# Weight tiles of one decoder layer, placed at set distances modulo 256 bytes from the activation tiles

## The chip, the core and the metric

The kernel runs on one core of a Trainium2 chip. The metric is device time in microseconds. Before the change it is 843.34 us, the median of three runs from 843.05 to 843.76. The one profiled execution took 842.98 us; the span that its page and its trace show, from the first to the last instruction, is 840.8 us, and 2.2 us lie around it.

## The reference

One layer of a decoder on 512 tokens of width 1024, all in float32. It has three sublayers with residual adds, and a last norm:

```python
h = rms_norm(x, norm_mix)
q, k, v, u, gate_b, gate_c, g_a, g_b = split(h @ w_in)
o_a = stick_breaking_attention(q, k, v)             # 8 heads x 64
y_b = gate_b * causal_depthwise_conv(gate_c * u)    # 3 taps, 512 channels
x = x + (sigmoid(g_a) * (o_a @ w_a) + sigmoid(g_b) * (y_b @ w_b)) @ w_mix_out
x = x + memory_cross_attention(rms_norm(x), rms_norm(mem), w_q, w_kv, w_o)   # 4 heads, 256 memory tokens
gate, up = split(rms_norm(x) @ w_ffn_in)            # 2 x 2816
x = x + (silu(gate) * up) @ w_ffn_out
return rms_norm(x, norm_final)
```

## The kernel before

**How a product is made.** Activations are kept transposed, channels on the 128 partitions and tokens along the row. Each float32 operand is split into a high and a low part, both in the matmul type float32r (`split` for activations, `halves`, `ffn_form` and `turn_form` for weights: ScalarE casts the high part, VectorE subtracts it). A product is then three matmuls: high by high, high by low, low by high (`mm3`, and the loop in `product`). Each matmul has a weight operand, 128 columns that are loaded into TensorE ahead of it, and a moving operand, which streams through. In the profile's rows `out<-moving,weights` stands for such a matmul, so `z<-xdh,wf` streams a tile `xdh` against weights `wf`; the instruction that loads the weights is the row of engine PEld with the same names.

**Two sizes.** Most plain products (`gemm`: the input projection `pr`, the branches `br`, the output projections `r` and `f`) stream 512 columns, all tokens of one part. The input half of the channel sublayer, the query projection of the memory sublayer, and four of the gate projections (`ffn_form`, `product`) use seven sums of 2 by 2 blocks in place of eight block products. Their matmuls stream 256 columns (`HS`), half of the tokens. There are 30 such units (22 of the channel sublayer, 4 of the query projection, 4 of the gates), each with seven products `i` = 0 to 6 of 4 slices by 3 matmuls: 84 matmuls a unit, 2,520 in all, all at line 802. The keys of the memory sublayer (`mem_k`) stream 256 columns too, the memory tokens: 8 calls of 8 slices by 3 matmuls, 192 in all. The products of `turn_form` and `turn_product` swap the roles: there the weight tile `tf` streams, 512 columns, and the activation forms are loaded.

**Where tiles lie.** Each pool takes a stretch of every partition's row. `upool` holds 52 units of 2,048 bytes: all activation parts `xgh`, `xoh`, `xch`, `acth` and so on. `wpool` holds four raw weights (`wr`), four high parts (`wh`) and four low parts (`wl`) of 4,096 bytes each; the block forms `wf` and `tf` use the buffers of `wh` and `wl`. `xpool` holds the forms `xdh` and `xdl` of the memory queries and of the channel sublayer; the gates' `xdh` and `xdl` are made by `pair_forms` with `split`, and so lie in `upool`. `lpool` holds the stick-breaking attention's `l` and `lq`, `cpool` the constants `ident`, `negtri`, `mean_r`. Start addresses in the built program, modulo 256 bytes:

| tiles | before | after the change |
|---|---|---|
| units in `upool` | 32 | 128 |
| `wh`, `wl` in `gemm`, `residual`, `mem_v`; `tf` | 32 | 128 |
| `wf` (block forms), `wh`, `wl` in `mem_k` | 32 | 192 |
| `xdh`, `xdl` in `xpool` | 64 | 128 |
| `l`, `lq` in `lpool` | 64 | 128 |
| `ident`, `negtri`, `mean_r` in `cpool` | 128 | 128 |

Slices of a tile start at multiples of 512 bytes, so each row of the table holds for all slices. Below, the distance of a matmul is the address of its weights less that of its moving operand, modulo 256. Counted over the built program, the 2,712 matmuls of line 802 and of `mem_k` divide before the change into 2,088 at distance 0 and 624 at distance 224, that is 32 bytes the other way (the 26 units whose `xdh` and `xdl` lie in `xpool`, 2 products of 12 matmuls each). Nearly all matmuls of 512 columns have distance 0 (2,022 of 2,062).

**What sets the order.** TensorE's order is written out by hand nearly everywhere (`manual_schedule`), in most of the kernel that of VectorE and ScalarE too. A form is made six products ahead of its use (`AHEAD`), its raw sums two more (`SUM_AHEAD`).

Of the kernel before, what the change touches and what calls it, by code (L numbers as in the profile page):

```python
# [8 lines left out]
F32 = mybir.dt.float32  # L9
F32R = mybir.dt.float32r  # L10
# [3 lines left out]
P = 128  # L14
D = 1024
S = 512
KD = D // P
TT = S // P
# [28 lines left out]
WARM = 8  # L47
FIRST = 4
LOADS_AHEAD = 6

O_Q, O_K, O_V, O_U, O_GB, O_GC, O_A, O_B = 0, 512, 1024, 1536, 2048, 2560, 3072, 4096

# [2 lines left out]
def hybrid_layer(ctx: ExitStack, tc: tile.TileContext, xT_d, memT_d, cols_d, wv_d, win_d,  # L55
# [3 lines left out]
    cpool = ctx.enter_context(tc.tile_pool(name="cpool", bufs=1))  # L59
    upool = ctx.enter_context(tc.tile_pool(name="upool", bufs=52))  # L60
    wpool = ctx.enter_context(tc.tile_pool(name="wpool", bufs=4))
    tpool = ctx.enter_context(tc.tile_pool(name="tpool", bufs=7))
    spool = ctx.enter_context(tc.tile_pool(name="spool", bufs=4))
# [9 lines left out]
    def nm(s):  # L73
        count[0] += 1
        return f"{s}{count[0]}"

    def unit(s, cols=512):
        return upool.tile([P, cols], F32R, tag="u", name=nm(s), padded_shape=[P, 512])

    def tmp(s, cols=512):  # L80
        return tpool.tile([P, cols], F32, tag="t", name=nm(s), padded_shape=[P, 512])

    def f(ap):
        return ap.bitcast(F32)

    def mmtile(s, pool=None, tag="mm"):
        return (pool or pmm).tile([P, 512], F32, tag=tag, name=nm(s))
# [21 lines left out]
    mean_r = cpool.tile([P, P], F32R, tag="mean_r", name="mean_r")  # L109
    nc.vector.tensor_copy(mean_r, mean_f)  # L110
    mean_sq = f(mean_r)
    eps_t = cpool.tile([P, 1], F32, tag="eps_t", name="eps_t", padded_shape=[P, 16])
    nc.vector.memset(eps_t, EPS)

    late_loads, n_loads = [], [0]
# [3 lines left out]
    def after(i, earlier):  # L119
        for e in earlier:  # L120
            tc.add_manual_dep(i.ins, e.ins.name, mybir.DependencyInfo(
                mybir.DependencyClass.NoSync, mybir.DependencyReason.DATA), reason="order")
# [28 lines left out]
    def chained(i):  # L151

        after(i, chain[-1:])
        chain.append(i)

    def load_w(src, cols=P):

        w, rest = halves(load_raw(src), D // cols)
        rest()
        return w  # L160

    def load_raw(src):
        raw = wpool.tile([P, D], F32, tag="wr", name=nm("wr"))
        i = nc.sync.dma_start(raw, src)
        loads[:] = [i]
        n_loads[0] += 1
        if n_loads[0] == LOADS_AHEAD + 1:
            after(i, late_loads[3:4])
        if count[1] < FIRST:
            count[1] += 1  # L170
            chained(i)
        return raw

    def halves(raw, k=KD):
        hi, lo = (wpool.tile([P, k, D // k], F32R, tag=t, name=nm(t)) for t in ("wh", "wl"))
        h2, l2 = (t.rearrange("p k c -> p (k c)") for t in (hi, lo))
        after(nc.scalar.copy(h2, raw), lead[-1:] + waiting[:1])  # L177

        def rest():
            lows.append(nc.vector.tensor_tensor(out=l2, in0=raw, in1=f(h2), op=ALU.subtract))  # L180
            after(lows[-1], waiting[1:])

        return (hi, lo), rest
# [6 lines left out]
    def gemm(ps, w, act, k0=0, ks=None):  # L190

        n = len(act)
        for k in ks or range(n):
            mm3(ps, (w[0][:, k0 + k, :], w[1][:, k0 + k, :]), act[k], k == 0, k == n - 1)
# [39 lines left out]
    def by_token_of(row, s):  # L234

        n = row.shape[1] // P
        r = cpool.tile([P, n, 32], F32, tag=s, name=nm(s))
        for g in range(TT):
            rows = slice(32 * g, 32 * g + 32)
            nc.vector.transpose(out=r[rows, :, :],  # L240
                                in_=row.rearrange("p (t c) -> p t c", c=P)[rows, :, rows])
        return r[:, :, 0]
# [20 lines left out]
    with tc.manual_schedule(engines={mybir.EngineType.Activation, mybir.EngineType.DVE}):  # L263
        for k in range(KD):
# [3 lines left out]
            if k == 0:  # L268
                hi, lo = unit("wvh"), unit("wvl")
# [36 lines left out]
    r0 = by_token_of(r0b, "r0")  # L306
# [9 lines left out]
    def open_project(col):  # L316
        w = load_w(win_d[col // P])
        ps = mmtile("pr")
        gemm(ps, w, xg, ks=range(KD // 2))
        opened.append((ps, w))  # L320
# [346 lines left out]
    def residual(w_dram, act, old, gain):  # L667
# [9 lines left out]
        def weight(m):  # L677
            if m not in raw:
                weight_raw(m)
            w[m], rest = halves(raw.pop(m))  # L680
            late.append(rest)
# [5 lines left out]
        def block(m, k0, k1, bank=mmtile):  # L687
            if k0 == 0:
                if m not in w:
                    w[m] = load_w(w_dram[m])  # L690
                ps[m] = bank("r")
            for k in range(k0, k1):
                mm3(ps[m], (w[m][0][:, k, :], w[m][1][:, k, :]), act[k], k == 0, k == KD - 1)
            if k1 == KD:
                finish(m)
# [39 lines left out]
    FORM_TAGS = "wh", "wl"  # L735
# [20 lines left out]
    def ffn_raw(m, i, eng=nc.vector):  # L756
        if m not in raws:
            ffn_load(m)
        w = raws[m]
        if w[i] is None:  # L760
            w[i] = fpool.tile([P, 512], F32, tag="w2", name=nm("s2"), bufs=4)
            a, b = (w[2], w[0]) if i == 3 else (w[3], w[1])
            eng.tensor_tensor(out=w[i], in0=a, in1=b, op=ALU.add)
        return w[i]

    wforms, made = {}, [0]

    def ffn_form(m, i, later=None):

        if (m, i) in wforms:  # L770
            return
        if i == 0:
            ffn_raw(m, i)
            pair = pairs[m]
            hi, lo = (wpool.tile([P, 2, 512], F32R, tag=t, name=nm("wf")) for t in FORM_TAGS)
            nc.scalar.copy(hi, pair)  # L776

            def rest():
                nc.vector.tensor_tensor(out=lo, in0=pair, in1=f(hi), op=ALU.subtract)  # L779

            if later is None:
                rest()
            else:
                later.append(rest)
            for j in range(2):
                wforms[m, j] = hi[:, j, :], lo[:, j, :]
            return
        raw = ffn_raw(m, i)
        w = wpool.tile([P, 2, 512], F32R, tag=FORM_TAGS[made[0] % 2], name=nm("wf"))
        made[0] += 1  # L790
        hi, lo = wforms[m, i] = w[:, 0, :], w[:, 1, :]
        nc.scalar.copy(hi, raw)  # L792
        nc.vector.tensor_tensor(out=lo, in0=raw, in1=f(hi), op=ALU.subtract)  # L793
# [139 lines left out]
    for n in range(GATE_AHEAD):  # L933
        ffn_form(*gs[n])
    with tc.manual_schedule(engines={mybir.EngineType.PE, mybir.EngineType.Activation,
# [7 lines left out]
        for n, (m, i) in enumerate(gs):  # L943
# [6 lines left out]
            if n + GATE_AHEAD < len(gs):  # L950
                ffn_form(*gs[n + GATE_AHEAD])
# [78 lines left out]
    km, vm, mq, scs, prs, pts = [], [[None] * 2 for _ in range(MT)], {}, {}, {}, {}  # L1030

    def mem_k(m):
        w = load_w(wmk_d[m])
        ps = mmtile("km")
        gemm(ps[:, :MEM], w, mg)
        t = tmp("km", MEM)
        nc.vector.tensor_tensor(out=t, in0=ps[:, :MEM], in1=rmb, op=ALU.mult)
        if m % 2 == 0:
            km_pair[:] = unit("kmh"), unit("kml")
        hi, lo = (u[:, (m % 2) * MEM:(m % 2 + 1) * MEM] for u in km_pair)  # L1040
        nc.scalar.copy(hi, t)
        nc.vector.tensor_tensor(out=lo, in0=t, in1=f(hi), op=ALU.subtract)
        km.append((hi, lo))
# [76 lines left out]
    with tc.manual_schedule(engines={mybir.EngineType.PE}):  # L1120
        for part, *args in ((mem_q, 0), (mem_k, 0), (mem_k, 1), (mem_scale,), (mem_k, 2), (mem_k, 3),
                            (mem_q, 1), (mem_scores, 0), (mem_k, 4), (mem_k, 5), (mem_scores, 1),
                            (mem_q, 2), (mem_k, 6), (mem_k, 7), (mem_turn, 0), (mem_v, 0),
                            (mem_turn, 1), (mem_scores, 2), (mem_q, 3), (mem_out, 0), (mem_out, 1),
                            (mem_v, 1), (mem_turn, 2), (mem_scores, 3), (mem_out, 2),
                            (last, 0, 0, 6), (last, 1, 0, 2), (mem_turn, 3), (last, 1, 2, 6),
                            (mem_out, 3), (last, 2, 0, 6, otile), (last, 0, 6, 8), (last, 1, 6, 8),
                            (last, 2, 6, 8)):
            part(*args)
        for m in range(3, KD):  # L1130
            last(m, 0, KD)
# [5 lines left out]
    def evict(m, part):  # L1137
# [6 lines left out]
        else:  # L1144
            a = act[m] = f(unit("act"))
            for half, u in enumerate((b["z"][:, :HS], b["t"][:, HS:])):
# [11 lines left out]

    rms, eps_sq = f(unit("rms")), cpool.tile([P, S], F32, tag="cu", name="eps_sq",
                                                 bufs=2, padded_shape=[P, S + 2])  # L1160
    eps_t4 = spool.tile([P, TT], F32, tag="epst", name="epst", bufs=1)
    eps_d = cpool.tile([P, P], F32, tag="eps_d", name="eps_d")
    yt = {}

    def turn_residual(t, h):
# [134 lines left out]

    def turn_form(p, i):

        w = wpool.tile([P, 2, 512], F32R, tag=FORM_TAGS[made[0] % 2], name=nm("tf"))
        made[0] += 1
        hi, lo = tforms[p, i] = w[:, 0, :], w[:, 1, :]
        nc.scalar.copy(hi, turn_raws[p][i])
        nc.vector.tensor_tensor(out=lo, in0=turn_raws[p][i], in1=f(hi), op=ALU.subtract)

    for k in range(TURN):
        w = load_w(wfo_d[k], D)  # L1310
# [63 lines left out]
    sums4 = {}  # L1374

    def small(s, cols=1):
        return spool.tile([P, cols], F32, tag=s, name=nm(s))

    def mean_part(t, j):

# [27 lines left out]
    rest = []  # L1408
# [123 lines left out]
```

## Time and profile before

| | |
|---|---|
| median of three runs | 843.34 us |
| profiled execution | 842.98 us |
| its span | 840.8 us |
| TensorE busy (weight loads apart) | 832.2 us, 5,077 matmuls |
| weight loads (PEld) | 744.9 us |
| VectorE busy | 678.3 us |
| ScalarE busy | 484.5 us |

In the page a row's time is the mean duration of one matmul, from when it starts to when its last result is out, and matmuls overlap: a matmul of 512 columns lasts 390 ns in these rows while the next one starts 227 ns after it. What one matmul costs is therefore read from the starts in the timeline, as a difference over several matmuls.

### The profile page before, as it was taken

The page shows a single profiled execution, that of the slowest core. Times are in us where ns is not written, and L with a number is a line of the kernel's source. Part 1 is how long each engine was busy: PE and PEld are TensorE (multiplying, and loading weights), DVE is VectorE, ACT ScalarE, POOL GpSimd, SP SyncE. Part 2 cuts the span into 40 slices and gives each one's busy share as a digit, 9 for nine tenths or more (in the row PEclk, how much of TensorE's full clock was granted, in tenths as well). Part 3 has the DMA queues.
Part 4 walks back from the last instruction along what each step waited for, and adds up shares of the span by engine and source line. Part 5 has one row for each costly group of instructions (what it writes and reads, how often), then busy time and mean ns, then how long its engine had stood idle before and what let it go on. Part 6 is the DMA issues. An engine that isn't in the chain of part 4 may idle for free.

```text
span 840.8 us, 13447 instructions
## 1 busy us (share of the span) xinstructions
PE 832.2 (99%) x5077; PEld 744.9 (89%) x5077; DVE 678.3 (81%) x1172; ACT 484.5 (58%) x874; POOL 85.2 (10%) x111
## 2 busy tenths in 40 slices
PE   9999999999999999999999999999999999999996
PEld 7888788888899988999988889999999999888885
DVE  8779889988866867988765889888877778889865
ACT  7466767666534555766554766555555556464534
POOL 1011112210100011000000111211111110010002
PEclk9999999999999999999999999999999999999999
DMA  8342232315645485565331437777777673881002
GB/s 301 108 144 82 95 101 72 105 51 183 192 110 141 155 241 152 142 182 195 129 112 62 113 81 206 185 184 183 180 176 176 176 176 113 266 273 51 1 1 101
DMA packets 50000, 119.67 MB, mean 142 GB/s; under 512 B 5136, under 2 KB 8208, under 8 KB 49936
## 3 DMA queue, kind: packets, MB, share of 16 engines
q1 hardware_dynamic: 40672, 101.23, 36.2%
q0 software_dynamic: 8976, 17.30, 12.4%
q8 instruction: 40, 0.66, 0.3%
q10 hardware_dynamic: 288, 0.29, 0.1%
q14 instruction: 24, 0.20, 0.1%
HBM read 115.63 MB, written 2.10 MB: 140 GB/s over the span
## 4 chain that ended last, share of the span: by engine, by line
PE 98%; DVE 1%; ACT 1%; issue 0%; DVEq 0%; ACTq 0%
PE z L802 20%; PE y L802 10%; PE pr L186 6%; PE pr L187 6%; PE pr L188 6%; PE v L802 5%; PE r L187 3%; PE r L186 3%; PE r L188 3%; PE v L302 3%; PE f L186 2%; PE f L188 2%; PE f L187 2%; PE t L188 2%; PE t L186 2%; PE t L187 2%
## 5 line engine op out<-in xcount | busy, mean ns | idle before, releaser
L177 ACT CAST wh<-wr 128x1024 fp32r<-128x1024 f32 x80 | 83.5, 1049 | 56.3 <-PE pr L187 10.1
L180 DVE TENSOR_TENSOR wl<-wr,wh 128x1024 fp32r<-128x1024 f32 x80 | 97.3, 1220 | 17.8 <-ACT wh L177 17.1
L802 PE MATMUL z<-xdh,wf 128*128 128x256 f32 x480 | 94.6, 281 | 0.0
L186 PE MATMUL pr<-xgh,wh 128*128 128x512 f32 x224 | 87.5, 391 | 0.0
L187 PE MATMUL pr<-xgl,wh 128*128 128x512 f32 x224 | 87.3, 390 | 0.0
L188 PE MATMUL pr<-xgh,wl 128*128 128x512 f32 x224 | 87.3, 390 | 0.0
L802 PEld LDWEIGHTS z<-xdh,wf 128*128 128x128 f32 x480 | 77.5, 189 | 0.2
L802 PE MATMUL z<-xdl,wf 128*128 128x256 f32 x240 | 67.0, 279 | 0.0
L826 ACT COPY sa<-z 128x256 f32<-128x256 f32 x52 | 19.4, 373 | 73.2 <-PE z L802 73.2
L793 DVE TENSOR_TENSOR wf<-s,wf 128x512 fp32r<-128x512 f32 x60 | 41.4, 692 | 22.6 <-ACT wf L792 21.4
L752 POOL DMA_DIRECT2D ws<-in_w_ffn_in_dram x22 | 26.5, 1206 | 299.7 <-DMA ws<-in_w_ffn_in_dram 123.6
L779 DVE TENSOR_TENSOR wf<-wg,wf 128x1024 fp32r<-128x1024 f32 x30 | 36.8, 1226 | 17.9 <-ACT wf L776 17.9
L188 PEld LDWEIGHTS pr<-xgh,wl 128*128 128x128 f32 x224 | 42.1, 188 | 8.8
L186 PEld LDWEIGHTS pr<-xgh,wh 128*128 128x128 f32 x224 | 42.1, 188 | 8.5 <-DVE rv L141 0.2
L187 PEld LDWEIGHTS pr<-xgl,wh 128*128 128x128 f32 x224 | 42.1, 188 | 8.3
L802 PE MATMUL y<-xch,wf 128*128 128x256 f32 x240 | 49.0, 286 | 0.0
L802 PE MATMUL z<-xch,wf 128*128 128x256 f32 x240 | 48.1, 283 | 0.0
L802 PEld LDWEIGHTS z<-xdl,wf 128*128 128x128 f32 x240 | 45.4, 189 | 0.2
L793 DVE TENSOR_TENSOR wf<-ws,wf 128x512 fp32r<-128x512 f32 x60 | 41.0, 683 | 1.8 <-ACT wf L792 1.7
L802 PE MATMUL v<-xoh,wf 128*128 128x256 f32 x208 | 42.0, 283 | 0.0
L802 PE MATMUL z<-xf,wf 128*128 128x256 f32 x312 | 41.8, 283 | 0.0
L802 PE MATMUL y<-xoh,wf 128*128 128x256 f32 x208 | 41.8, 284 | 0.0
(359 smaller groups left out, 2479.7 us busy)
## 6 DMA issues: line engine op xcount, KB each, us to landing
wr<-in_w_in_dram SPq DMA_DIRECT2D x28, 512.0 KB, 3.6
ws<-in_w_ffn_in_dram SPq DMA_DIRECT2D x22, 512.0 KB, 3.9
ws<-in_w_ffn_in_dram POOLq DMA_DIRECT2D x22, 512.0 KB, 5.8
wg<-in_w_ffn_in_dram SPq DMA_DIRECT2D x22, 512.0 KB, 4.3
wr<-in_w_ffn_out_dram SPq DMA_DIRECT2D x12, 512.0 KB, 7.3
a<-in_w_ffn_in_dram SPq DMA_DIRECT2D x22, 256.0 KB, 4.6
wr<-in_w_branch_dram SPq DMA_DIRECT2D x8, 512.0 KB, 3.4
wr<-in_w_mix_out_dram SPq DMA_DIRECT2D x8, 512.0 KB, 3.6
```

The costliest lines, as they stand in the source:

```text
L177: after(nc.scalar.copy(h2, raw), lead[-1:] + waiting[:1])
L180: lows.append(nc.vector.tensor_tensor(out=l2, in0=raw, in1=f(h2), op=ALU.subtract))
L186: nc.tensor.matmul(ps, a[0], b[0], start=start, stop=False, **kw)
L187: nc.tensor.matmul(ps, a[0], b[1], start=False, stop=False, **kw)
L188: nc.tensor.matmul(ps, a[1], b[0], start=False, stop=stop, **kw)
L302: nc.tensor.matmul(vps[t], xg[k][a][:, sl], wv[k][b], start=k == 0 and (a, b) == (0, 0), stop=k == KD - 1 and a == 1)
L752: nc.gpsimd.dma_start(s13, a[:, 0:4:3, :], accum_op=ALU.add)
L779: nc.vector.tensor_tensor(out=lo, in0=pair, in1=f(hi), op=ALU.subtract)
L793: nc.vector.tensor_tensor(out=lo, in0=raw, in1=f(hi), op=ALU.subtract)
L802: nc.tensor.matmul(ps[:, :HS], a, b, start=i < 3 and k == 0 and j == 0, stop=k == KP - 1 and j == 2, skip_group_check=True)
L826: nc.scalar.copy((s[:, :HS], None, None, s[:, HS:], t[:, :HS], t[:, :HS])[i], z)
```

## The change

It adds a constant `SHIFT` of 16 elements, 64 bytes. `wtile` allocates the split weights with room for it (4,352 bytes a buffer, so that all buffers keep the same address modulo 256) and starts the tile either at the buffer's start or 64 bytes behind. The plain weights and `tf` take 0; the block forms `wf` and the weights of `mem_k` take 64 bytes. Some small tiles are padded or share a buffer (`eps_t`, `eps_d` in the buffer of `r0`, `epst`, `fy` in that of `ry`), which moves `upool`, `wpool`, `tpool`, `lpool`, `xpool`, `fpool` and `gpool` to 128 modulo 256. The result is the right column of the table above: all 2,712 matmuls of line 802 and of `mem_k` have distance 64, and all matmuls of 512 and 384 columns distance 0.

No instruction is added, removed or moved: on each of the five engines the built program has the same instructions in the same order, with the same tiles and the same waits, and only addresses differ.

```diff
--- before.py
+++ after.py
@@ -47,6 +47,7 @@
 WARM = 8
 FIRST = 4
 LOADS_AHEAD = 6
+SHIFT = 16
 
 O_Q, O_K, O_V, O_U, O_GB, O_GC, O_A, O_B = 0, 512, 1024, 1536, 2048, 2560, 3072, 4096
 
@@ -109,7 +110,7 @@
     mean_r = cpool.tile([P, P], F32R, tag="mean_r", name="mean_r")
     nc.vector.tensor_copy(mean_r, mean_f)
     mean_sq = f(mean_r)
-    eps_t = cpool.tile([P, 1], F32, tag="eps_t", name="eps_t", padded_shape=[P, 16])
+    eps_t = cpool.tile([P, 1], F32, tag="eps_t", name="eps_t", padded_shape=[P, 40])
     nc.vector.memset(eps_t, EPS)
 
     late_loads, n_loads = [], [0]
@@ -153,9 +154,9 @@
         after(i, chain[-1:])
         chain.append(i)
 
-    def load_w(src, cols=P):
-
-        w, rest = halves(load_raw(src), D // cols)
+    def load_w(src, cols=P, shift=0):
+
+        w, rest = halves(load_raw(src), D // cols, shift)
         rest()
         return w
 
@@ -171,8 +172,12 @@
             chained(i)
         return raw
 
-    def halves(raw, k=KD):
-        hi, lo = (wpool.tile([P, k, D // k], F32R, tag=t, name=nm(t)) for t in ("wh", "wl"))
+    def wtile(tag, s, k, shift):
+        w = wpool.tile([P, D + SHIFT], F32R, tag=tag, name=nm(s), padded_shape=[P, D + 64])
+        return w[:, shift:shift + D].rearrange("p (k c) -> p k c", k=k)
+
+    def halves(raw, k=KD, shift=0):
+        hi, lo = (wtile(t, t, k, shift) for t in ("wh", "wl"))
         h2, l2 = (t.rearrange("p k c -> p (k c)") for t in (hi, lo))
         after(nc.scalar.copy(h2, raw), lead[-1:] + waiting[:1])
 
@@ -772,7 +777,7 @@
         if i == 0:
             ffn_raw(m, i)
             pair = pairs[m]
-            hi, lo = (wpool.tile([P, 2, 512], F32R, tag=t, name=nm("wf")) for t in FORM_TAGS)
+            hi, lo = (wtile(t, "wf", 2, SHIFT) for t in FORM_TAGS)
             nc.scalar.copy(hi, pair)
 
             def rest():
@@ -786,7 +791,7 @@
                 wforms[m, j] = hi[:, j, :], lo[:, j, :]
             return
         raw = ffn_raw(m, i)
-        w = wpool.tile([P, 2, 512], F32R, tag=FORM_TAGS[made[0] % 2], name=nm("wf"))
+        w = wtile(FORM_TAGS[made[0] % 2], "wf", 2, SHIFT)
         made[0] += 1
         hi, lo = wforms[m, i] = w[:, 0, :], w[:, 1, :]
         nc.scalar.copy(hi, raw)
@@ -1030,7 +1035,7 @@
     km, vm, mq, scs, prs, pts = [], [[None] * 2 for _ in range(MT)], {}, {}, {}, {}
 
     def mem_k(m):
-        w = load_w(wmk_d[m])
+        w = load_w(wmk_d[m], shift=SHIFT)
         ps = mmtile("km")
         gemm(ps[:, :MEM], w, mg)
         t = tmp("km", MEM)
@@ -1158,8 +1163,8 @@
 
     rms, eps_sq = f(unit("rms")), cpool.tile([P, S], F32, tag="cu", name="eps_sq",
                                                  bufs=2, padded_shape=[P, S + 2])
-    eps_t4 = spool.tile([P, TT], F32, tag="epst", name="epst", bufs=1)
-    eps_d = cpool.tile([P, P], F32, tag="eps_d", name="eps_d")
+    eps_t4 = spool.tile([P, TT], F32, tag="epst", name="epst", bufs=1, padded_shape=[P, 28])
+    eps_d = cpool.tile([P, P], F32, tag="r0", name="eps_d")
     yt = {}
 
     def turn_residual(t, h):
@@ -1300,7 +1305,7 @@
 
     def turn_form(p, i):
 
-        w = wpool.tile([P, 2, 512], F32R, tag=FORM_TAGS[made[0] % 2], name=nm("tf"))
+        w = wtile(FORM_TAGS[made[0] % 2], "tf", 2, 0)
         made[0] += 1
         hi, lo = tforms[p, i] = w[:, 0, :], w[:, 1, :]
         nc.scalar.copy(hi, turn_raws[p][i])
@@ -1374,7 +1379,8 @@
     sums4 = {}
 
     def small(s, cols=1):
-        return spool.tile([P, cols], F32, tag=s, name=nm(s))
+        return spool.tile([P, cols], F32, tag="ry" if s == "fy" else s, name=nm(s),
+                          padded_shape=[P, TT] if s == "fy" else None)
 
     def mean_part(t, j):
```

## The prediction

> **What bounds the kernel now.** The first view is the profile's page: span, busy time by engine, the chain of work that ended last, and the clock.
>
> ```profile
> span 840.8 us, 13447 instructions
> PE 832.2 (99%) x5077; PEld 744.9 (89%) x5077; DVE 678.3 (81%) x1172; ACT 484.5 (58%) x874; POOL 85.2 (10%) x111
> PE 98%; DVE 1%; ACT 1%; issue 0%; DVEq 0%; ACTq 0%
> PEclk9999999999999999999999999999999999999999
> ```
>
> TensorE is busy for 832.2 of 840.8 us, holds 98% of the chain, and its clock is granted in full from end to end. So the time is the sum of what each of the 5,077 matmuls takes until the next may start, and a change that leaves order and waits alone can only act on that step. The second view is therefore TensorE's timeline, read from start to start. First eight matmuls of 512 columns:
>
> ```profile
> 99.94 0.39 PE L186 MATMUL pr<-xgh,wh 128*128 128x512 f32 x1
> ...
> 101.75 0.39 PE L188 MATMUL pr<-xgh,wl 128*128 128x512 f32 x1
> ```
>
> 1.81 us for eight is 226 ns each. These have distance 0 before and after, so the term of all plain products, `tf` included, stays as it is. Next a stretch of the channel sublayer. Each product has 12 matmuls of 256 columns, and the rows are the first of each product:
>
> ```profile
> 562.22 1.60 PE L802 MATMUL z<-xf,wf 128*128 128x256 f32 x12
> ...
> 565.10 0.28 PE L802 MATMUL v<-xoh,wf 128*128 128x256 f32 x1
> ...
> 566.53 0.28 PE L802 MATMUL z<-xdh,wf 128*128 128x256 f32 x1
> ...
> 567.95 0.28 PE L802 MATMUL y<-xch,wf 128*128 128x256 f32 x1
> ...
> 569.39 0.28 PE L802 MATMUL y<-xoh,wf 128*128 128x256 f32 x1
> ...
> 570.83 0.28 PE L802 MATMUL z<-xdh,wf 128*128 128x256 f32 x1
> ...
> 572.25 1.60 PE L802 MATMUL z<-xf,wf 128*128 128x256 f32 x12
> ```
>
> The two products with `xch` and `xoh`, from 567.95 to 570.83, take 2.88 us for 24 matmuls, 120.0 ns each, at distance 0. The products with `xdh` take 1.42 us for 12, both times: 118.3 ns each, at distance 224. Is it the address, or the product? The gates have the same product, with `xdh` among the units, so at distance 0:
>
> ```profile
> 239.03 0.28 PE L802 MATMUL z<-xdh,wf 128*128 128x256 f32 x1
> ...
> 240.47 0.28 PE L802 MATMUL z<-xgh,wf 128*128 128x256 f32 x1
> ```
>
> 1.44 us for 12, 120.0 ns. The same code is 1.7 ns a matmul slower where both tiles lie alike modulo 256. The memory keys stand at 120 too:
>
> ```profile
> 382.43 0.28 PE L186 MATMUL km<-mgh,wh 128*128 128x256 f32 x1
> ...
> 384.35 0.28 PE L187 MATMUL km<-mgl,wh 128*128 128x256 f32 x1
> ```
>
> 1.92 us for 16 steps. So the distance between weights and moving operand has a price in this trace, a small one in the one case that it shows. The Trainium skill speaks against that, and so against this change: its page "TensorE: Matmul & The Clock Gate", Part 2: What happens when you issue a matmul, says that loading the next weights takes no read bandwidth from the running matmul since the two have ports of their own, and "SBUF — State Buffer", Who interferes with whom, that TensorE waits on nobody. By that rule no address matters and the time stays at 843.3 us; the pair of 118.3 and 120.0 ns does not agree with it, though 1.7 ns is little to go by.
>
> **The change part by part.** Nothing is added, removed or reordered on any engine, and no wait changes, so no queue is passed and no instruction stands behind a new one. What is left is the step of each matmul, in three groups.
>
> *The 2,712 matmuls of 256 columns that go to distance 64.* That is line 802 with 2,520 and the keys with 192; 2,088 of them come from 120.0 ns, 624 from 118.3. What a step at distance 64 takes is the unknown, and the trace hardly shows it. The floor comes from matmuls that stream only two columns, where nothing but the loading of weights sets the pace:
>
> ```profile
> 386.42 0.25 PE L219 MATMUL var<-mean_r,accl 128*128 128x2 f32 x1
> ...
> 387.09 0.25 PE L219 MATMUL var<-mean_r,accl 128*128 128x2 f32 x1
> ```
>
> Six steps in 0.67 us are 112 ns. Each of the 2,712 loads weights of its own, so none can go below 112. The other end comes from the only pair of this size that has distance 64 before, in the attention:
>
> ```profile
> 84.63 0.63 PE L428 MATMUL z<-lq,qkh 128*128 128x512 f32 x2
> 85.10 0.40 PE L428 MATMUL z<-lq,qkl 128*128 128x512 f32 x1
> 85.33 0.40 PE L479 MATMUL z<-l,negtri 128*128 128x256 f32 x2
> 85.57 0.40 PE L507 MATMUL o<-ah,v 128*128 128x512 f32 x1
> ```
>
> The two with `negtri` take 0.24 us; with each stamp rounded to 0.01 that is between 115 and 125 ns a step, and 125 is the upper end. (The first rows show 0.47 us for two of 512 columns at distance 224, 235 ns each, where the input projection has 226: for that size leaving distance 0 gains nothing and may cost 9.) Between 112 and 125 I take 117. The nearest row with many matmuls behind it is the 118.3 of the products with `xdh`, the only ones long enough to settle at a distance other than 0. That they gain 1.7 ns with 32 bytes makes a gain likelier than a loss, and 64 bytes is twice as far; so a little under 118.3, and not the floor.
>
> Worked out: 2,088 x (120.0 - 117) = 6.3 us, and 624 x (118.3 - 117) = 0.8 us, 7.1 us less. At the ends, 112 ns gives 2,088 x 8.0 + 624 x 6.3 = 20.6 us less, and 125 ns gives 2,088 x 5.0 + 624 x 6.7 = 14.6 us more. The Trainium skill, "TensorE: Matmul & The Clock Gate", Back-to-back issue gap, has 256 / 2.4 + 2.5 ns, 109 ns, as the step of a matmul of this size by itself; at that the estimate would be 28 us less, but the 112 ns of the weight loads stand above it here.
>
> *What goes to distance 0.* 40 matmuls of 512 and 16 of 384 columns of the attention (`l`, `lq`, the mean over `mean_r`) come from other distances. At the 9 ns above, 0 to 0.5 us less. The 22 of 256 columns beside them run at about 120 already. Against it 64 transposes with `ident` and 8 matmuls with `mean_r` come to distance 0 as well; where 128 columns stream at distance 0 in the attention, the step is
>
> ```profile
> 93.42 0.28 PE L507 MATMUL o<-al,v 128*128 128x128 f32 x1
> 93.53 0.27 PE L507 MATMUL o<-ah,v 128*128 128x128 f32 x1
> 93.64 0.27 PE L507 MATMUL o<-al,v 128*128 128x128 f32 x1
> ```
>
> 110 ns, about the floor, so 0 to 0.3 us more. I count both together as nothing.
>
> *The other engines.* They get other addresses too. Whether VectorE or ScalarE runs differently there is not in the trace; what hides it is TensorE's load. The tightest stretch for them is the channel sublayer:
>
> ```profile
> 540.00:600.00 60.00, 60.00 (x505) 60.00 (x504) 51.08 (x91) 31.54 (x60) 7.25 (x6) 1.00 0.73 185
> ```
>
> The columns are the stretch, its length, then busy time of PE, PEld, DVE, ACT and POOL, clock, DMA share and GB/s. VectorE is busy for 51.08 of 60 us. If every step fell to 112 ns, the same work would have 60 x 112 / 119.4 = 56.3 us (119.4 is a whole unit of the rows above: 84 matmuls in the 10.03 us from 562.22 to 572.25), and VectorE would be at 91%. Below 100%, so this cover holds even at the floor. If it did not, each us of VectorE beyond it would come back as a wait of TensorE. Tiles that share a buffer now (`eps_d`, `fy`) come long after the last reader of the buffer's first tile, and no wait is added for them.
>
> The sum is 842.98 - 7.1 = 835.9 us against the profiled execution. The median of the runs shown is 0.4 us above that execution, so the forecast is **836.2 us**, 0.85% less.
>
> **The rivals.**
>
> *The floor is reached.* If at distance 64 the stream and the load no longer get in each other's way, only the 112 ns remain, and the time is 843.3 - 20.6 = 822.7 us. For it: 64 bytes is farther than the 32 of `xdh`, and at 112 VectorE still keeps up. Against it: 512 columns also show 226 ns, well over the floor of a load, at distance 0, so a part of a step may be no conflict at all.
>
> *Distance does nothing.* Then the 118.3 ns of `xdh` belong to something else that `xpool` has, and the steps stay between 118.3 and 120.0 or return to 120.0: 843.3 to 844.4 us (624 x 1.7 = 1.1). That the change doesn't do what it says is this same case. For it: 0.24 us for the pair at distance 64, just 120. Against it: the gates' `xdh` at 120.0. The ports as the Trainium skill has them on "SBUF — State Buffer", Who interferes with whom, would give this case too.
>
> *Slower: the load meets the stream at a worse point.* At distance 64 the stream catches up with the load's address early in each matmul instead of starting on it, and is held up once more than at 0. Price: half way between 120 and 125, 122.5 ns, so 2,088 x 2.5 + 624 x 4.2 = 7.8 us more, 851.1 us. For it: the 235 ns of 512 columns off distance 0. Against it: the 118.3. It decides from a step of 119.6 ns on, where 2,088 x 0.4 less and 624 x 1.3 more cancel.
>
> **How the numbers follow.** Forecast, steps from about 114.5 to 119 ns: 0.48. Floor, 112 to 114.5: 0.17. Nothing, 119 to 120.5: 0.17. Slower, above: 0.18. A measurement of this kernel can tell about 0.2%, 1.7 us, from no change; 119 ns is 1.7 us less and 120.5 about 2.4 us more, so these cases are also faster (0.48 + 0.17), same (0.17) and slower (0.18). The floor's 822.7 is the lower end, since only small savings elsewhere lie below. Upward the range reaches 848, about 121.3 ns, and leaves out the worse half of the slower case, some 0.1; with a little below the lower end that is under 0.2.
>
> **What would show it.** In the profile after, a product of 12 matmuls at line 802 takes 1.40 us from its first row to the next product's first (1.34 to 1.35 at the floor, 1.44 if distance does nothing, 1.47 if it hurts), and products with `xdh` take as long as the others; eight steps of `pr` still take 1.81 us; VectorE's and ScalarE's busy totals stay at 678 and 485 us. The prediction is wrong if the step differs between `xdh` and the rest, if `pr` leaves 226 to 227 ns (then the address itself counts, not only the distance), or if TensorE's busy share falls (then another engine waits).

## The result and the profile after

The changed kernel takes **833.23 us**, the median of four runs (832.21 to 835.46), beside 843.53 us before (843.05 to 843.76). The ratio is 0.9882, with a 95% interval from 0.9861 to 0.9904: 10.3 us less. The profiled execution took 833.82 us. Its page:

```profile
span 831.7 us, 13447 instructions
PE 822.6 (99%) x5077; PEld 735.2 (88%) x5077; DVE 679.2 (82%) x1172; ACT 484.0 (58%) x874; POOL 86.0 (10%) x111
PEclk9999999999999999999999999999999999999998
```

The span is 9.1 us shorter, TensorE's busy time 9.6 us; VectorE and ScalarE worked as long as before (678.3 and 484.5 us), and TensorE is still busy 99% of the span, with the clock at nine tenths or more in all slices but the last. So the steps of the matmuls became shorter and nothing else. Plain products kept theirs, as the timeline shows for eight matmuls of 512 columns:

```profile
99.97 0.39 PE L191 MATMUL pr<-xgh,wh 128*128 128x512 f32 x1
...
101.79 0.39 PE L193 MATMUL pr<-xgh,wl 128*128 128x512 f32 x1
```

1.82 us for eight, 227.5 ns each. Now the channel sublayer. The timeline merges the twelve matmuls of a product with `xf` into one row, from its first start to its last end; the last matmul alone lasts 0.28 us, so (length - 0.28) / 11 is the step. Before, this row was 1.60 us long, 120 ns a step. After:

```profile
558.06 1.58 PE L807 MATMUL z<-xf,wf 128*128 128x256 f32 x12
...
562.30 0.28 PE L807 MATMUL z<-xdh,wf 128*128 128x256 f32 x1
...
563.72 0.28 PE L807 MATMUL y<-xch,wf 128*128 128x256 f32 x1
...
567.96 1.58 PE L807 MATMUL z<-xf,wf 128*128 128x256 f32 x12
```

A whole unit, 84 matmuls, takes 9.90 us, 117.9 ns each, and the product with `xdh` takes 1.42 us, no longer less than its neighbours. But 74 us later, in the same execution, at the same distance of 64 bytes:

```profile
636.32 0.28 PE L807 MATMUL z<-xdh,wf 128*128 128x256 f32 x1
...
637.68 1.52 PE L807 MATMUL z<-xf,wf 128*128 128x256 f32 x12
```

Here the product with `xdh` takes 1.36 us and the row of `xf` is 1.52 us long, 113 ns a step. Read over all starts of the trace, there are **two lasting steps**, 117.7 ns and 113.4 ns, each held for up to hundreds of matmuls, with little between. TensorE's time divides as follows, each matmul counted from its start to the next one's:

| us | before | after |
|---|---|---|
| 2,712 matmuls of line 802 (807) and of the keys | 325.0 | 315.8 |
| 1,248 matmuls with plain weights, 512 columns | 284.6 | 284.6 |
| all others | 222.3 | 222.3 |

All of the 9.2 us comes out of the first row: 119.8 ns a matmul before, 116.45 after, of which 1,174 steps are of the short kind (115 ns or less) and 1,507 of the long (116 to 119).

### The profile page after: what moved, and what is told of

Same layout as the page of the kernel before. It is cut to its first block, busy times and chain, and to the rows that moved or that the text cites. A ratio compares the mean times of both kernels' runs of the same rounds, so it can differ in the third digit from the quotient of the medians.

```text
span 831.7 us, 13447 instructions
## 1 busy us (share of the span) xinstructions
PE 822.6 (99%) x5077; PEld 735.2 (88%) x5077; DVE 679.2 (82%) x1172; ACT 484.0 (58%) x874; POOL 86.0 (10%) x111
## 4 chain that ended last, share of the span: by engine, by line
PE 97%; DVE 1%; ACT 1%; DMA 1%; issue 0%; SPq 0%; DVEq 0%; ACTq 0%
PE z L807 20%; PE y L807 10%; PE pr L191 6%; PE pr L192 6%; PE pr L193 6%; PE v L807 5%; PE r L193 3%; PE r L192 3%; PE r L191 3%; PE v L307 2%; PE f L193 2%; PE f L191 2%; PE f L192 2%; PE t L193 2%; PE t L191 2%; PE t L192 2%
## 5 line engine op out<-in xcount | busy, mean ns | idle before, releaser
L807 PE MATMUL z<-xdh,wf 128*128 128x256 f32 x480 | 92.8, 279 | 0.0
L757 POOL DMA_DIRECT2D ws<-in_w_ffn_in_dram x22 | 26.5, 1206 | 292.4 <-DMA ws<-in_w_ffn_in_dram 113.4
```

Of the source, the lines that this page charges most:

```text
L757: nc.gpsimd.dma_start(s13, a[:, 0:4:3, :], accum_op=ALU.add)
L807: nc.tensor.matmul(ps[:, :HS], a, b, start=i < 3 and k == 0 and j == 0, stop=k == KP - 1 and j == 2, skip_group_check=True)
```

## The experiments

Two questions were open: whether the distance does it, or the new addresses as such, and what chooses between 117.7 and 113.4 ns. Mean steps in this part are taken from the starts of all matmuls in a trace; where rows stand beside them, they can be read there.

**All at distance 0**, with the new pools and padding kept:

```diff
-SHIFT = 16
+SHIFT = 0
```

> The changed kernel with SHIFT = 0: the same pools and padding (units at 128 modulo 256), but the block forms and the keys' weights at distance 0 again. Theory (the distance of weights and stream sets the step): every matmul at line 807 and of the keys takes 120.0 ns, the products with xdh too, which lose their 118.3; 843 to 845 us. Rival (the gain comes from the new addresses themselves, 128 instead of 32 modulo 256): steps stay at 113 to 118 ns and the time at 833 us.

Measured 844.83 us (844.24 to 845.34, ten runs) beside 843.59, ratio 1.0014 (1.0005 to 1.0024). Its timeline in the channel sublayer:

```profile
553.58 1.60 PE L807 MATMUL z<-xf,wf 128*128 128x256 f32 x12
...
563.66 1.60 PE L807 MATMUL z<-xf,wf 128*128 128x256 f32 x12
```

120 ns again: 10.08 us for a unit of 84, and 2,569 of the 2,712 steps in its trace are 120 ns. The new addresses alone gain nothing. The 1.2 us above the kernel before is what the forecast counted for the loss of the products with `xdh` (624 x 1.7 ns = 1.1 us): their 118.3 ns were a matter of distance too.

**Eight distances, in rising and in falling order.**

```diff
+SWEEP = (0, 8, 16, 24, 32, 40, 48, 56)    # falling: (56, 48, ..., 0)
...
+    def swept(m):
+        return SWEEP[m // 3] if m < NF else SHIFT
...
-            hi, lo = (wtile(t, "wf", 2, SHIFT) for t in FORM_TAGS)
+            hi, lo = (wtile(t, "wf", 2, swept(m)) for t in FORM_TAGS)
...
-            w[m], rest = halves(raw.pop(m))
+            w[m], rest = halves(raw.pop(m), KD, SWEEP[m])
```

> The changed kernel, but the block forms of the channel sublayer's units 0-2, 3-5, ... 21 stand at distances 0, 32, 64, ... 224 bytes, and the weights of the two output projections (512 columns) of blocks 0 to 7 at the same eight distances. Theory (distance): the steps of each group of units follow its distance: 120.0 ns at 0, 118 at 224, 113 to 118 at 64, and 512 columns take 227 ns at 0 and more elsewhere. Rival (what counts is how TensorE enters a stretch, since the profile after shows 113.4 and 117.7 ns at the same distance 64, 113.4 mostly where the transposes of the residual stand between): units 11 to 18 run at 113.4 whatever their distance, the others at 117.7 to 120. Time 830 to 845 us by either.

> The same sweep with the distances in falling order: 224 in units 0-2 down to 0 in unit 21, and 224 to 0 over the blocks of the output projections. Theory (distance): each distance shows the step that it showed in the rising sweep, though it stands elsewhere. Rival (the entry): the step belongs to the place, 113.4 ns in units 11 to 18 in both sweeps. If both count, a distance shows two lasting steps, and the transposes choose between them.

Single times of 840.40 and 841.31 us. Mean steps in ns, rising / falling (at 64 bytes the column of 256 columns holds the gates, queries and keys as well):

| distance, bytes | 256 columns | 512 columns |
|---|---|---|
| 0 | 120.0 / 120.1 | 227.2 / 227.6 |
| 32 | 118.4 / 119.4 | 234.9 / 233.1 |
| 64 | 117.1 / 117.6 | 233.5 / 233.4 |
| 96 | 119.5 / 119.4 | 233.9 / 234.3 |
| 128 | 119.8 / 118.8 | 233.5 / 233.1 |
| 160 | 120.8 / 119.9 | 233.4 / 233.5 |
| 192 | 115.6 / 117.8 | 229.3 / 231.5 |
| 224 | 117.9 / 118.1 | 233.4 / 233.3 |

Some of these means hold a few steps that stand at an interruption and not in the stream. Three steps of about 200 ns, one behind each group of transposes, lift 128, 160 and 192 in the rising order and 32 and 96 in the falling one by 1 ns; a few such steps lift 64 by 0.7 in both, and one of over 310 ns lifts the 512 columns at 32 (rising) and 192 (falling) by 2 ns.

The distance sets the step wherever the group stands, so the rival falls in its plain form: in the rising sweep units 12 to 17, at 128 and 160 bytes, stood at 119.8 and 120.8 ns in spite of the transposes. For 512 columns 0 is best in both sweeps. For 256 columns no distance is clearly slower than 0 once these steps are left out (160 is then at 119.8 and 119.9 ns, 0 at 119.8), and 64 and 192 are the two that keep the short step: there up to 259 and 82 steps of 113 or 114 ns follow one another, at the six others no two. Those two have different means in the two orders, since a stretch there is at the one step or at the other. At 192, for one:

```profile
694.05 1.52 PE L811 MATMUL z<-xf,wf 128*128 128x256 f32 x12
```

in the rising sweep, where the units at 192 stand late, and in the falling one, where they stand early:

```profile
542.46 1.57 PE L811 MATMUL z<-xf,wf 128*128 128x256 f32 x12
```

**A finer sweep.** As above, with `SWEEP = (10, 12, 14, 18, 20, 22, 44, 52)`, and for the plain weights a tuple of their own, `(2, 4, 6, 58, 60, 62, 44, 52)`.

> The changed kernel with the block forms of units 0-2, 3-5, ... 21 at distances 40, 48, 56, 72, 80, 88, 176 and 208 bytes, and the plain weights of blocks 0 to 7 of the output projections at 8, 16, 24, 232, 240, 248, 176 and 208. Theory (reads meet in pieces of some width, so what counts is the piece): distances close to 64 or 192 show the same two steps of 113.4 and 117.7, and 512 columns keep 227 ns within some bytes of 0. Rival (only the exact distance counts): 118 to 120 ns everywhere but at 64 and 192, and 230 to 236 everywhere but at 0. Time 830 to 845 us by either.

839.66 us, once. The blocks' mean steps at 40, 48, 56, 72, 80, 88, 176 and 208 bytes are 119.5, 118.1, 117.8, 118.3, 119.8, 115.9, 119.1 and 117.6 ns; 512 columns at 8, 16, 24, 232, 240 and 248 take 230.8, 235.2 (233.3 without one step of over 310), 230.4, 231.1, 228.3 and 233.2, and at 176 and 208 bytes 230.1 and 231.9. So the rival is the closer one: already 8 bytes off 0 cost 512 columns 3 to 6 ns, and near 64 the short step is mostly gone. Of the new distances 88 shows it too, in about 60% of its matmuls, and its mean of 115.9 ns is below the 117.3 of the gates, queries and keys, which stood at 64 in this run; no run has 88 throughout. Pieces of some width don't explain that; what does stays open.

**The plain weights at 64 too**, against the split of the change:

```diff
-    def load_w(src, cols=P, shift=0):
+    def load_w(src, cols=P, shift=None):
...
-        w, rest = halves(load_raw(src), D // cols, shift)
+        w, rest = halves(load_raw(src), D // cols, (SHIFT if cols == P else 0) if shift is None else shift)
...
-            w[m], rest = halves(raw.pop(m))
+            w[m], rest = halves(raw.pop(m), KD, SHIFT)
```

> The changed kernel with the weights of the plain products of 512 columns (input projection, branches, output projections: 672 + 192 + 384 = 1,248 matmuls) at distance 64 too. If 512 columns suffer as the attention's rows before the change let fear (235 against 226 ns): up to 1,248 x 9 = 11 us more, 844 us, and the split of the change is right. If distance has no effect on 512 columns: 833 us. If they gain as 256 columns do (3 to 7 ns): 825 to 829 us, and the split gives time away.

Measured 839.71 us (839.13 to 842.14), ratio 0.9959 (0.9943 to 0.9976). Eight matmuls of the input projection in its timeline:

```profile
99.95 0.39 PE L191 MATMUL pr<-xgh,wh 128*128 128x512 f32 x1
...
101.82 0.39 PE L193 MATMUL pr<-xgh,wl 128*128 128x512 f32 x1
```

1.87 us for eight, 234 ns each where distance 0 has 227.5. The 1,248 matmuls take 292.3 us instead of 284.6, 7.7 us more, and the kernel is some 6.5 us behind the changed one; its blocks, at 115.55 ns in this profile, gained a little meanwhile. So of these two distances the split has the right one for each: 512 columns are faster at 0, 256 columns at 64.

**Four idle transposes in units 2 and 6.**

```diff
+IDLE = {2: 4, 6: 4}
...
+    def idle_turns(n):
+        ps = mmtile("dm")
+        for j in range(n):
+            nc.tensor.transpose(ps[:, j * P:(j + 1) * P], ident, ident)
...
+            elif i == 5 and m in IDLE:
+                idle_turns(IDLE[m])
```

> The changed kernel with four idle transposes (ident by ident into a bank of their own, nothing reads them) in units 2 and 6 of the channel sublayer, at the place where units 11 to 18 transpose the residual. In the profile after, 740 matmuls in a row ahead of unit 11 took 117.7 ns and those behind the transposes 113.4, at the same distance of 64 bytes. Theory (at 64 bytes there are two lasting steps, and an interruption of TensorE's stream chooses between them; four transposes choose the short one): units 2 to 10, some 720 matmuls, run at 113.4, 3.1 us less, and each group of transposes costs about 0.45 us, so 2.2 us less than the changed kernel, 831.0 us. Rival (the short step in units 11 to 18 comes from something else of that place, such as less work on the other engines): the steps of units 2 to 10 stay at 117.7, and the time rises by 0.9 us to 834.1.

Measured 832.23 us (831.42 to 832.82) beside 842.97 us for the kernel before on that chip: 0.9870 (0.9853 to 0.9886), not apart from the changed kernel's 0.9882. Its profile shows units 2 to 10 at 113.4, as the theory has it, and the time of the 2,712 at 313.6 instead of 315.8 us. It doesn't show that the transposes chose that step: the 142 matmuls ahead of the first group stood at 113.4 already, and the repeat below keeps that step there without any transposes. That the time shows less than the forecast 2.2 us fits the repeat below: the changed kernel itself runs at the short step there in some executions.

**One to four idle transposes**, with `IDLE = {1: 1, 2: 2, 3: 3, 4: 4, 5: 1, 6: 2, 7: 3, 8: 4, 9: 1, 10: 2}`.

> The changed kernel with one, two, three, four idle transposes in units 1, 2, 3, 4, again one to four in units 5 to 8, and one and two in 9 and 10. In the profile after, the one group of a single transpose is followed by 117.7 ns, the eight groups of four by 113.4. Theory (the interruption's length chooses the step): units behind one transpose run at 117.7, behind four at 113.4, and two and three side with the one or the other each time alike. Rival (chance chooses): the same count is followed by different steps. Time 830 to 837 us by either.

834.99 us, once. Its timeline, the idle transposes (`dm`) and the `xf` product that follows:

```profile
515.57 0.27 PE L1184 MATMUL dm<-ident 128*128 128x128 f32 x1
...
519.92 1.58 PE L808 MATMUL z<-xf,wf 128*128 128x256 f32 x12
...
525.58 0.38 PE L1184 MATMUL dm<-ident 128*128 128x128 f32 x2
...
529.90 1.52 PE L808 MATMUL z<-xf,wf 128*128 128x256 f32 x12
...
555.20 0.27 PE L1184 MATMUL dm<-ident 128*128 128x128 f32 x1
...
559.55 1.58 PE L808 MATMUL z<-xf,wf 128*128 128x256 f32 x12
...
565.21 0.38 PE L1184 MATMUL dm<-ident 128*128 128x128 f32 x2
...
569.54 1.52 PE L808 MATMUL z<-xf,wf 128*128 128x256 f32 x12
```

One transpose is followed by the long step (units 1, 5, 9), two, three or four by the short one (units 2, 3, 4, 6, 7, 8, 10), ten of ten. Six of these ten changed the step: the single ones came on a stream at 113.4 and left it at 117.7, the pairs the other way round. There the interruption chooses. The groups of three and four came on a stream at 113.4 and left it there; that four turn the long step into the short one is seen once, behind unit 11 in the first profile. It is no rule for every place, though: behind the single transpose of unit 19 stood the long step in the first profile and the short one in this run.

**The changed kernel once more, and pairs of transposes at five places.** The second adds `idle_turns(2)` at the gates' start, behind two of their branches, in unit 1 of the queries and unit 2 of the channel sublayer, and a second transpose in `turn_eps`.

> The changed kernel once more, as it stands, on the same chip as its variants. Theory (two lasting steps, chosen by how each interruption falls): 831 to 836 us, with a spread of some us between its runs, where the kernel before spreads by about 1 us; in its profile other stretches may stand at 117.7 and 113.4 than in the first one. Rival (one profile's steps hold for all runs): the same stretches at the same steps, and a spread of about 1 us.

> The changed kernel with two idle transposes at five places (the gates' start and behind two of their branches, unit 1 of the memory queries, unit 2 of the channel sublayer) and a second transpose beside the single one of unit 19. In the run with counts, one transpose was followed by 117.7 ns three times of three and two or more by 113.4 seven times of seven, and a pair cost about 0.23 us. Theory (a pair chooses the short step until the next interruption): some 270 matmuls of the gates and up to 1,100 of the queries and the channel sublayer that stood at 117.7 go to 113.4, 1.2 to 5.4 us less, at a cost of 1.3 us; against the changed kernel on the same chip between 0.1 us more and 4 us less, and a narrower spread of its runs. Rival (the choice isn't governed by the pairs there, since the next wait undoes it): 1.3 us more.

The repeat measured 831.61 us (830.63 to 835.41, five runs), 0.9868 (0.9850 to 0.9886); with pairs it is 831.56 (831.46 to 831.76), 0.9860 (0.9846 to 0.9873), beside 843.51 before. Two stretches of 60 us of the channel sublayer, ahead of the residual's transposes and among them (the columns as in the prediction), in the first profile of the changed kernel:

```profile
540.00:600.00 60.00, 60.00 (x512) 60.00 (x511) 50.99 (x91) 31.97 (x62) 7.94 (x7) 1.00 0.76 190
625.00:685.00 60.00, 60.00 (x532) 60.00 (x531) 47.86 (x85) 34.85 (x67) 7.23 (x6) 1.00 0.74 185
```

and the first of them in the repeat:

```profile
540.00:600.00 60.00, 60.00 (x532) 60.00 (x531) 52.60 (x93) 33.32 (x65) 8.45 (x7) 1.00 0.76 195
```

512 matmuls in one, 532 in the other: the same instructions at the same addresses, at the long step in one execution and at the short one in the next. In the first profile the long step sets in where TensorE was held up for an instant, at 525.4:

```profile
525.29 0.28 PE L807 MATMUL y<-xch,wf 128*128 128x256 f32 x1
525.45 0.38 PE L807 MATMUL y<-xoh,wf 128*128 128x256 f32 x1
525.67 0.28 PE L807 MATMUL y<-xol,wf 128*128 128x256 f32 x1
525.79 0.40 PE L807 MATMUL y<-xoh,wf 128*128 128x256 f32 x2
```

Steps of 160 and 220 ns, where 113 stood before them and 118 behind, for the next 740 matmuls. The repeat has no such hold there. VectorE's rows of the first profile point to what TensorE waited for:

```profile
524.99 0.41 DVE L841 TENSOR_TENSOR sb<-y,sb 128x256 f32<-128x256 f32 x1
```

This reads unit 2's `y` until 525.40, and the matmul at 525.45 is the first one that adds to that `y` again. In the repeat the same read ended 0.18 us ahead of its matmul, before the change 0.86 us. So with the shorter steps TensorE caught up with VectorE at this point. A hold alone does not decide the step, though: the run with the plain weights at 64 has one at the same place (182 and 222 ns, the read again 0.06 us ahead), and its next 740 matmuls stayed at 113.4.

At 4.3 ns a matmul, the 898 that stand between two interruptions here make 3.9 us, which is about the spread: five runs of the changed kernel lie 4.8 us apart, the four with pairs 0.3 us. No profile of the slowest run shows it, so this is argued. In its middle the version with pairs is no faster, since its transposes cost about what they gain. And behind the branches its pairs failed: 82 and 106 matmuls followed at 117.7.

**Pairs inside the stream.** The last run moved those two pairs one product on:

```diff
-            if (m, i) == (GM, 2):
+            if (m, i) in ((GM, 2), (GM + 1, 3), (GM + 2, 3)):
                 idle_turns(2)
...
-                if m < last_m - 1:
-                    idle_turns(2)
```

> As the run with pairs of transposes at five places, but in the gates the two pairs that stood right behind a branch (24 matmuls of 512 columns) stand one product later, between matmuls of 256 columns. Behind the branches the pairs were followed by 117.7 ns twice (81 and 104 matmuls), while the pair at the gates' start, between matmuls of 256 columns, was followed by 113.4. Theory (a pair chooses the short step only where the stream of 256 columns already runs): behind the moved pairs 113.4 ns for the some 70 and 95 matmuls that follow up to the next branch, 0.7 us less than that run, 830.8 us beside a kernel before of 843.5. Rival (in these two places the step is 117.7 for another reason): 117.7 as before, 831.6 us.

Measured **830.91 us** (830.23 to 833.33, five runs) beside 843.92, ratio 0.9852 (0.9838 to 0.9866). Its timeline behind the first moved pair:

```profile
255.90 0.38 PE L939 MATMUL dm<-ident 128*128 128x128 f32 x2
...
257.49 0.28 PE L807 MATMUL z<-xch,wf 128*128 128x256 f32 x1
...
258.85 0.28 PE L807 MATMUL v<-xgh,wf 128*128 128x256 f32 x1
```

1.36 us for twelve, the short step, and 68 and 91 matmuls hold it to the next branch. The theory holds in both places. This version has the lowest ratio of all, and 2,166 short steps of 2,712, but its interval overlaps that of the changed kernel (0.9850 to 0.9886 in the repeat), so that it is faster than that one is not settled by time. One of its runs, at 833.33, lies 2.4 us above its median, so the pairs don't hold the spread down each time either.

**Distance 192 throughout**, with `SHIFT = 48`:

> The changed kernel with SHIFT = 48, so that the block forms and the keys' weights stand at distance 192 in place of 64. In the sweeps only 64 and 192 of the eight distances showed steps of 113.4 and 117.7 alone. Theory (a distance is as good as its steps): 113.4 and 117.7 and nothing between, 831 to 837 us. Rival (the sweeps' short stretches at 192 stood by chance where the step is short): 118 to 120 ns, 838 to 844 us.

838.51 us (834.82 to 839.30), ratio 0.9931 (0.9910 to 0.9953). The rival is nearer: 2,628 of 2,712 steps are long ones, also behind the residual's transposes, and 56 short. At 192 the same two steps exist, but here four transposes were followed by the long one all eight times, where in the rising sweep, at the same distance, four were followed by the short one behind units 17 and 18. What decides there stays open. One of its four runs, at 834.82, may have held the other step; it has no profile.

## Why the prediction was right, point by point

- **The time is the sum of TensorE's steps, and only those of the 2,712 matmuls change.** Right: these lost 9.2 us, all other matmuls nothing, and the other engines' busy times stayed.
- **The distance sets the step, not the address itself.** Right, and shown: with the same pools at distance 0 nearly all steps are 120 ns (2,569 of 2,712). The two rows on which this rested, 118.3 and 120.0 ns for one product in two places, pointed the right way. The rule of the Trainium skill ("SBUF — State Buffer", Who interferes with whom), by which TensorE waits on nobody, would leave no room for this, and the runs do not agree with it: the distance alone took the 2,712 matmuls from 326.8 us in the run at 0 to 315.8 us. Why load and stream meet so, no run shows.
- **117 ns a step at distance 64.** The size that was off, and the form. The mean is 116.45 ns in the first profile, 115.28 in the repeat, so the term of 7.1 us was 9.2 and 12.4. Worse, there is no such step: it is 117.7 or 113.4, and each execution mixes them in its own way. A product of twelve takes 1.42 or 1.36 us, not the 1.40 of the prediction. That 117 came out near the mean is luck in part. Its reason, that 64 bytes is twice as far as the 32 of `xdh`, failed: 96, 128 and 160 bytes, farther still, stand at 118 to 121 ns in the sweeps. The forecast of 836.2 us is near what the long step alone would give (325.0 us less 2,712 x 117.7 ns is 5.8 us, so 837.5).
- **The floor of 112 ns.** Sound: the short step stands 1.4 ns above it, and no distance lasted below 113.4. VectorE kept up over a whole stretch at the short step, with 52.60 of 60 us busy, but not at every point in it: its read at 525.40 came back as a wait of TensorE, the kind that the prediction named for a cover that fails, 0.05 us in the first of the two long steps (160 ns in place of 113).
- **512 columns keep 226 to 227 ns, and leaving distance 0 may cost 9.** Right: the 1,248 plain matmuls took 284.6 us before and after (the 227.5 ns of the eight rows is 1.82 us beside 1.81, a matter of rounding), and the cost is 6 ns on average at 64.
- **The rivals.** "Distance does nothing" falls with the run at 0, "slower" with the result. "The floor is reached" came true in part, for 1,174 of 2,712 steps in the first profile and 2,037 in the repeat.

## What to carry to other kernels

Where TensorE is never idle, its time is a sum of steps, and the step of matmuls that each load new float32 weights can depend on where weights and stream lie modulo 256 bytes: compare the starts of the same product in two places before taking a matmul's price as given. Sweep the distance separately for each width, by giving groups of one loop different distances in a single kernel; what is best for 512 columns cost 256 columns 2 to 6%, and the other way round 3%. And where a step can settle at two values, look at several executions before comparing two versions, since a single profile shows only one mix.

## What was not expected of the hardware

At distances of 64 and 192 bytes a stream of 256-column matmuls settles at 113.4 or at 117.7 ns and keeps that for up to 898 matmuls in a row, until something interrupts it. An instant's hold (160 and 220 ns) turned one into the other for 87 us in one run; one of 182 and 222 ns at the same place in another run did not. In the channel sublayer one idle transpose turned the short step into the long one and two turned it back; two right behind a branch were followed by the long one. Which state of load and stream the two steps stand for, why just these distances have them, and why 8 bytes off 0 already cost 512 columns 3 to 6 ns, no run here shows.
